# Moving every on-chip pool so that TensorE's operand rows begin at multiples of 128 bytes

## The chip, the core and the metric

The kernel runs on one NeuronCore of a Trainium2 chip. The metric is device time in microseconds of one execution, as the median of several timed runs; lower is better. The other seven cores are idle.

Each core has five engines that run their own instruction streams and meet at semaphores: TensorE (PE; matrix products, out of the on-chip memory SBUF into PSUM), VectorE (DVE), ScalarE (ACT), GpSimd (POOL) and SyncE (SP), which here only issues transfers. SBUF has 128 partitions; a tile of the program takes the same stretch of bytes in each of them. "Where a row begins" means the byte address within a partition.

## The reference, cut to what is computed

One block of a hybrid model on 512 tokens of width 1024, all in float32:

```python
h = rms_norm(x, norm1_g)
z, xbc, dt_raw, q, k, v, g_ssd, g_attn = split(h @ w_in)            # 12832 columns
y_ssd  = ssd_branch(z, xbc, dt_raw, ...)     # conv, state space in chunks of 128, gated norm
y_attn = attn_branch(q, k, v, ...)           # dilations 1, 4, 16; 8 heads of 64 in each
merged = sigmoid(g_ssd) * (y_ssd @ w_ssd_proj) + sigmoid(g_attn) * (y_attn @ w_attn_proj)
x  = x + merged @ w_out
h2 = rms_norm(x, norm2_g)
u_gate, u_val = split(causal_dwconv(h2 @ w_up))                     # 2 x 2816 columns
out = x + (silu(u_gate) * u_val) @ w_down
```

## The kernel before

**Products in three parts.** A float32 product is made of three float32r products: every operand is split into a high part (a copy rounded to float32r) and a low part (what is left), and high x high, high x low and low x high are added up in PSUM. The names show it: hh/hl (the normed input, transposed), ah/al (attention out), yh/yl (state space out), mh/ml (merged), h2h/h2l (second norm), acth/actl (feed-forward), whi/wlo (weights). Weights come as a stream of 194 pieces of 128 x 1024: load_piece (L85) issues the transfer into raw, make_piece (L91) splits it with one ScalarE copy (L100) and one VectorE subtraction (L101).

**Two forms of product.** In mm_chan (L135) the weights are the stationary operand, 128 columns wide, and the activations stream past as the moving one, 512 columns: the products of ps_ssd, ps_gate, ps_ap and ps_u (L140). The state space out-projection ps_sp (L855) has that form too. In proj_tok (L387, products at L393: ps_v, ps_qk) and mm_tok (L876, products at L882: ps_wo, ps_wd) it is the other way round: the activations are stationary and 512 weight columns move. In the trace's names the moving operand comes first: ps_ssd<-hl,whi streams hl past whi. For the second and third dilation tok (L382) reads the activations with a step of 4 tokens.

**Order.** TensorE's order is written by hand (manual_schedule, L147): attention projections by dilation, 8 groups of the state space branch, gates, the projections of the two branches, the output projection with the second norm, then the feed-forward. The smaller work (attention scores and values, transposes, state space chains) goes on in generators, one step at a tick, a tick being 12 products (L143 to L145, L455). Its products are float32 ones, not float32r: ps_s (L496), ps_pt, ps_pv, ps_tq, ps_st, ps_y, ps_o.

**Placement.** Pools are stacks: those of the left side grow up from const, those of side="right" grow down from the top. Within a pool a tile takes its bytes per partition, rounded up to 32. In the program as built, by address and by what is left over a multiple of 128:

| tiles | first byte | past a multiple of 128 |
|---|---|---|
| ident, ones, wd2 (const) | 16512, 17024, 22272 | 0 |
| triu, tril, sc (const) | 17632, 18144, 18656 | 96 |
| raw, whi, wlo (weights, after const ends) | 24736, 37024, 49312 | 32 |
| hh, hl; mh, ml; yh, yl; acth, actl; bct, xst, zs (left) | 72352, 88736; ... | 32 |
| ah, al, ysb; x1, h2h, h2l (right, from the top 229344 down) | 212960, 221152, 180192; ... | 96 |
| s, pt, gt, hn, junk (right, below those) | 167904, 174048, ... | 96 |
| kz, qt, vt, qr, mneg (right, below res4; 32 bytes) | 135104, 114880, 106688, ... | 64 |
| sr, sq, prev, xdt, xdc, btok, cbm, eb, bc (right, below two rv; 32 bytes each) | 173984, ... | 32 |

The rows of a tile are whole multiples of 128 bytes apart, and the slices that TensorE reads begin at multiples of 512 bytes within a tile (the step of 4 tokens in tok excepted: there they begin 0, 4, 8 or 12 bytes on). So all rows of a tile share its remainder.

Of the kernel before, what the change touches and what calls it, by code (L numbers as in the profile page):

```python
# [8 lines left out]
F32 = mybir.dt.float32  # L9
# [7 lines left out]
P = 128  # L17
S = 512
NT = S // P
# [1 line left out]
KD = D // P  # L21
EPS = 1e-6
NEG = -1.0e30
# Ticks (of 12 matrix products) between the steps of the work beside the weight products.
LAG, PVLAG, QLAG = 2, 2, 4      # attention: scores to transposes, those to values, head norms
LW = (3, 0, 0)                  # further wait of the attention of each dilation
COMB = 11                       # last attention chain to the combination of the dilations
G0, G1, GN = (2, 1, 1, 1), (5, 2, 4, 2), (7, 2, 2)  # state space groups: C.B, inputs, outputs
G2W, YL = 4, 3
NL = (1, 3, 2, 1)               # steps of a group's norm  # L30

Z0, XS0, B0, C0, DT0 = 0, 2048, 4096, 5120, 6144
Q0, K0, V0, GS0, GA0 = 6176, 7712, 9248, 10784, 11808
# [5 lines left out]
def kernel(  # L39
# [6 lines left out]
    nc = tc.nc  # L46
    x, out = x[0], out[0]
# [6 lines left out]
    def pool(name, side="left", bufs=1):  # L54
        return tc.tile_pool(name=name, bufs=bufs, side=side, reuse_waits="tile")

    cp = ctx.enter_context(pool("const"))
# [4 lines left out]
    def bank(tag, name):  # L62
        return pp.tile([P, 512], F32, tag=tag, name=name, bufs={"mm": 4, "tr": 2, "aux": 2}[tag])

    # ---- weights: a stream of pieces of 128 x 1024, each split into two float32r parts
    def chan_piece(w, c0, n, k0=0, nk=KD):
        return w[k0 * P:(k0 + nk) * P, c0:c0 + n].rearrange("(k p) c -> p k c", p=P)

    pieces = []
# [15 lines left out]
    def load_piece():  # L85
        n = len(raws)
        raw = wp.tile([P, pieces[n].shape[1], pieces[n].shape[2]], F32, tag="raw", name=f"raw{n}", bufs=3)
        nc.sync.dma_start(raw, pieces[n])
        raws.append(raw)
# [22 lines left out]
            make_piece()  # L112
        return made[i]

    # ---- work beside the matrix products: generators that go on at each tick
    sides = []

    def tick():
# [9 lines left out]
    def start(gen, wait=0):  # L128
        sides.append([gen, wait])
# [47 lines left out]
    scr_r = dp.tile([8, S], F32, tag="scr_r", name="scr_r")  # L177
    scr_f = dp.tile([24, S], F32, tag="scr_f", name="scr_f")

    comb_cm = pool("comb")  # L180
    comb = comb_cm.__enter__()
    hT_cm = pool("hT")
# [11 lines left out]
    def wide(b):  # L194
        return ysb[:, b:b + 2, :].rearrange("p a b -> p (a b)")

    # ---- first norm
    def rstd(ss, rs, n):
        nc.vector.tensor_scalar(ss, ss, 1.0 / n, EPS, op0=ALU.mult, op1=ALU.add)  # L199
        nc.gpsimd.tensor_tensor(rs, ss, nhalf.broadcast_to(tuple(ss.shape)) if ss.shape[1] > 1 else nhalf, op=ALU.pow)  # L200
# [13 lines left out]
    for t in range(NT):  # L214
        nc.sync.dma_start(wide(2 * t), x[t * P:(t + 1) * P, :])
        if t < 2:
            load_piece()
    # keeps TensorE busy until the first operands are there, so that its clock is up by then
    def warm(n, name):
        ps = bank("tr", f"ps_warm{name}")  # L220
        for i in range(n):
            nc.tensor.matmul(ps[:, :P], ones, ones, start=True, stop=True)
# [28 lines left out]
    def first_l(t, half):  # L251
        rest[t, half]()

    # ---- parameters by channel, on partitions
    def params():
        r1, r2, r3, r4 = (ysb[:n, 12, i * P:(i + 1) * P] for i, n in enumerate((128, 108, 88, 44)))
        nc.sync.dma_start(r1, ssd_conv_w[0].rearrange("k (b p) -> (k b) p", p=P))
        o = 0
        for v, n in ((ssd_conv_b, 32), (norm1_g, 8), (ssd_norm_g, 16), (norm2_g, 8), (ffn_conv_b, 44)):
            nc.sync.dma_start(r2[o:o + n, :], v[0].rearrange("(b p) -> b p", p=P))  # L260
            o += n
        nc.sync.dma_start(r3, ffn_conv_w[0, 0:2].rearrange("k (b p) -> (k b) p", p=P))
        nc.sync.dma_start(r4, ffn_conv_w[0, 2].rearrange("(b p) -> b p", p=P))
        for j, v in enumerate((q_norm_g, k_norm_g)):
            for i in range(2):
                nc.sync.dma_start(qkg[i * 64:(i + 1) * 64, j:j + 1], v[0].unsqueeze(1))
        for i in range(2):
            nc.sync.dma_start(dsk[i * 64:(i + 1) * 64, :],
                              d_skip[0].rearrange("(b i) -> i b", i=2)[i].partition_broadcast(64))
        yield 3  # L270
        nc.gpsimd.tensor_scalar(qkg[:, 0:1], qkg[:, 0:1], 0.125, None, op0=ALU.mult)
        ps = bank("tr", "ps_sc")
        o = 0
        for r, n in ((r1, 128), (r2, 108), (r3, 88), (r4, 44)):
            nc.tensor.transpose(ps[:, o:o + n], r, ident[:n, :n])
            o += n
        nc.vector.tensor_copy(sc, ps[:, :368])

    # ---- time steps: softplus, decays and their running sums
    def time_steps():  # L280
        def small(i):
            return ysb[:, 13, i * P:(i + 1) * P] if i < 4 else ysb[:, 15, (i - 4) * P:(i - 3) * P]
# [71 lines left out]
    start(params(), 1)  # L354
    start(time_steps(), 7)

    # ---- dilated window attention
    aa_cm = pool("attn_a", side="right")
    aa = aa_cm.__enter__()
    ab_cm = pool("attn_b", side="right")  # L360
# [2 lines left out]
    def masks():  # L363
        for j, src in enumerate((triu, tril)):
            nc.vector.tensor_scalar(mneg[:, j, :], src, -NEG, NEG, op0=ALU.mult, op1=ALU.add)
        res4 = aa.tile([P, 4], F32, tag="res4", name="res4")
        nc.vector.reduce_sum(res4, ident.rearrange("p (a b) -> p b a", b=4), axis=AX.X)
        nc.vector.tensor_mul(mneg[:, 2, :].rearrange("p (a b) -> p a b", b=4),
                             tril.rearrange("p (a b) -> p a b", b=4),
                             res4.unsqueeze(1).broadcast_to((P, 32, 4)))  # L370
        nc.vector.tensor_scalar(mneg[:, 2, :], mneg[:, 2, :], -NEG, NEG, op0=ALU.mult, op1=ALU.add)
        yield 1
# [85 lines left out]
    def norm_heads(which, g, b, ps):  # L458
        nm = f"{which}_{g}_{b}"
        qr = ab.tile([P, 512], F32, tag="qr", name=f"qr{nm}", bufs=4)  # L460
        nc.scalar.copy(qr, ps)
        sq = ab.tile([P, 512], F32, tag="qsq", name=f"qsq{nm}", bufs=1)
        nc.scalar.activation(sq, qr, AF.Square)
        ss = ab.tile([P, 8], F32, tag="qss", name=f"qss{nm}", bufs=4)
        nc.vector.reduce_sum(ss, sq.rearrange("p (h d) -> p h d", h=8), axis=AX.X)
        rs = ab.tile([P, 8], F32, tag="qrs", name=f"qrs{nm}", bufs=4)
        rstd(ss, rs, 64)

        def later():
            q3 = qr.rearrange("p (h d) -> p h d", h=8)  # L470
            nc.vector.tensor_mul(q3, q3, rs.unsqueeze(2).broadcast_to((P, 8, 64)))
            yield 1
            ps = bank("tr", f"ps_tq{nm}")
            for j in range(4):
                nc.tensor.transpose(ps[:, j * P:(j + 1) * P], qr[:, j * P:(j + 1) * P], ident)
            p3 = ps.rearrange("p (j t) -> p j t", j=4)
            bs = slice(b * P, (b + 1) * P)
            if which == 0:
                nc.scalar.activation(qts[g % 2][:, :, bs], p3, AF.Copy, scale=qkg[:, 0:1])
            else:  # L480
                nc.scalar.activation(kz[0:64, :, 0, bs], p3[0:64], AF.Copy, scale=qkg[0:64, 1:2])
                nc.vector.tensor_scalar(kz[64:128, :, 1, bs], p3[64:128], qkg[64:128, 1:2], None, op0=ALU.mult)
        start(later(), QLAG)
# [3 lines left out]
    def chain(g, j, b, nb):  # L487
# [38 lines left out]
        if b + nb == NT:  # L526
# [5 lines left out]
            if j == 3:  # L532
# [4 lines left out]
                if g == 2:  # L537
                    start(combine(), COMB)

# [59 lines left out]
    for g in range(3):  # L599
# [5 lines left out]
        for which in (0, 1):  # L605
            proj_tok(g, f"qk{which}{g}_", lambda b, ps: norm_heads(which, g, b, ps))
        start(launch(g), QLAG + LW[g])
        if g == 2:
            proj_v()

    # ---- state space branch
    sa_cm = pool("ssd_a")
    late = {}

# [20 lines left out]
    def ssd_side(g, bct, xst, zs, at):  # L635
        sp = late["b"]

        def T(tag, shape, bufs=1):
            return sp.tile(shape, F32, tag=tag, name=f"{tag}_{g}", bufs=bufs)
# [77 lines left out]
        nc.gpsimd.tensor_add(sq[:, 0, :], sq[:, 0, :], sq[:, 1, :])  # L717
        yield NL[0]
        sr = sp.tile([P, 2, S], F32R, tag="sr", name=f"sr_{g}", bufs=1)
        nc.scalar.copy(sr[:, 0, :], sq[:, 0, :])  # L720
        nc.gpsimd.tensor_sub(sr[:, 1, :], sq[:, 0, :], sr[:, 0, :].bitcast(F32))
        yield NL[1]
        ps = bank("aux", f"ps_n{g}")
# [3 lines left out]
        nc.scalar.activation(vv, ps[0:1, :], AF.Identity, bias=epsb[0:1], scale=1.0 / 256)  # L727
        nc.sync.dma_start(scr_v[g], vv)
        yield NL[2]
        rv = T("rv", [P, NT], 2)  # L730
        nc.sync.dma_start(rv, scr_v[g].rearrange("(p c) -> p c", c=NT))
        yield NL[3]
        nc.gpsimd.tensor_tensor(rv, rv, nhalf.broadcast_to((P, NT)), op=ALU.pow)
# [14 lines left out]
    for g in range(8):  # L748
        if g > 1:
            branch_tiles(g)  # L750
        if g > 1:
            start(ssd_side(g, *tiles[g], normal), G2W if g == 2 else 0)
# [30 lines left out]
                start(ssd_side(1, *branch_tiles(1), dict(zip(("cb", "x", "y"), G1))), G1[3])  # L783
                start(silus(*tiles[0]), 1)

    # ---- gates and projections of the two branches
    def gate(m, o):
        w = next_piece()
        ps = bank("mm", f"ps_gate{m}")
# [75 lines left out]
    yp_cm.__exit__(None, None, None)  # L865
    ap_cm.__exit__(None, None, None)

    # ---- output projection, residual and second norm
    x1_cm = pool("x1", side="right")
    x1p = x1_cm.__enter__()  # L870
    x1 = x1p.tile([P, NT, D], F32, tag="x1", name="x1")
# [32 lines left out]
    n2 = np_cm.__enter__()  # L904
    gb2 = n2.tile([P, D], F32, tag="gb2", name="gb2")
    nc.sync.dma_start(gb2, norm2_g[0].partition_broadcast(P))
    sums = n2.tile([P, NT, 2], F32, tag="sums", name="sums")

    def add_x1(nh, b, ps):
        cs = slice(nh * 512, (nh + 1) * 512)  # L910
# [61 lines left out]
        for i in range(2):  # L972
            mm_chan(up0[i], wu[i], h2h, h2l, t0=256, nt=256, ticks=False, lo_first=True)

    # ---- feed-forward
    ff_cm = pool("ffn")
    act_cm = pool("act")

# [69 lines left out]
```

## Time and profile before

| what | value |
|---|---|
| timed runs, median (lowest to highest) | 1248.98 us (1247.35 to 1249.27) |
| span of the profiled execution, first to last instruction | 1246.2 us (its own time is not listed apart) |
| TensorE busy | 1228.4 us, 99%, 5944 products |
| VectorE / ScalarE / GpSimd busy | 57% / 45% / 8% |
| mean granted TensorE clock over the span | 0.995 |
| transfers | 128.11 MB, 16 engines busy 35% of the span |

How to read it: TensorE's products are pipelined, so that two that follow each other overlap in the trace, and the mean duration of one is not its pace. The chain that ended last gives each instruction only the time by which it moved the end, so that a long piece of the chain, divided by the number of its products, is the pace. Stages by time: attention projections up to 296 us, state space 297 to 629, gates to 723, ps_ap to 745, ps_sp to 832, ps_wo to 877, ps_u to 1123, ps_wd to the end.

### The profile page before, as it was taken

To read this page: it belongs to the slowest core of one execution; us is meant where nothing else is said; L and a number is where in the kernel's file an instruction comes from. 1 tells how busy PE (TensorE), PEld (TensorE's weight loads), DVE (VectorE), ACT (ScalarE), POOL (GpSimd) and SP (SyncE) were. 2 spreads that over 40 slices of the span, in tenths; PEclk is the share of its full clock that TensorE was granted. 3 is DMA by queue.
4 is the path that set the end of the run, shared out by engine and by line. 5 is a ranking of instruction groups with operands and counts; after the bars stand their busy time and mean duration, and the time that the engine had idled before them with its cause. 6 is when DMAs were issued, how large, how long until landed. Compare 5 with 4: busy or idle time off the path is not lost.

```text
span 1246.2 us, 15060 instructions
## 1 busy us (share of the span) xinstructions
PE 1228.4 (99%) x5944; PEld 1025.2 (82%) x5944; DVE 713.2 (57%) x956; ACT 557.6 (45%) x848; POOL 95.1 (8%) x71
## 2 busy tenths in 40 slices
PE   8799999999999999999999999999999999999998
PEld 6579888898788888888888888888888888888887
DVE  4255455655588988777743553653766566563222
ACT  3334454646766555655433233432544444442210
POOL 2022022220000101110102000000000000000000
PEclk9899999999999999999999999999999999999999
DMA  4333212113445644344333523343233332332340
GB/s 158 106 85 88 69 52 69 51 53 85 131 125 162 182 116 123 100 135 118 86 81 89 167 86 102 101 170 101 85 98 89 102 98 88 102 100 87 110 127 34
DMA packets 154829, 128.11 MB, mean 103 GB/s; under 512 B 12662, under 2 KB 125926, under 8 KB 153735
## 3 DMA queue, kind: packets, MB, share of 16 engines
q1 hardware_dynamic: 154759, 127.15, 34.9%
q8 instruction: 47, 0.77, 0.3%
q14 instruction: 23, 0.19, 0.1%
HBM read 124.72 MB, written 2.41 MB: 102 GB/s over the span
## 4 chain that ended last, share of the span: by engine, by line
PE 90%; DVE 3%; DMA 3%; ACT 1%; POOL 1%; issue 1%; SPq 0%; DVEq 0%; POOLq 0%; ACTq 0%
PE ps_u L140 19%; PE ps_ssd L140 18%; PE ps_qk L393 10%; PE ps_wd L882 10%; PE ps_gate L140 7%; PE ps_sp L855 7%; PE ps_v L393 5%; PE ps_wo L882 3%; PE ps_s L496 2%; PE ps_ap L140 2%; PE ps_pv L523 1%; PE ps_pt L512 1%; PE ps_y L703 1%; DMA ysb<-in_w_in_dram 1%; PE ps_o L708 1%; DMA dsk<-in_d_skip_dram 1%
## 5 line engine op out<-in xcount | busy, mean ns | idle before, releaser
L101 DVE TENSOR_TENSOR wlo<-raw,whi 128x1024 fp32r<-128x1024 f32 x194 | 244.1, 1259 | 330.4 <-ACT whi L100 204.6
L100 ACT CAST whi<-raw 128x1024 fp32r<-128x1024 f32 x194 | 203.3, 1049 | 319.5 <-PE ps_wd L882 79.8
L140 PE MATMUL ps_ssd<-hl,whi 128*128 128x512 f32 x384 | 103.4, 398 | 0.0
L140 PE MATMUL ps_ssd<-hh,whi 128*128 128x512 f32 x384 | 98.6, 399 | 0.0
L140 PE MATMUL ps_ssd<-hh,wlo 128*128 128x512 f32 x384 | 95.3, 390 | 0.0
L140 PE MATMUL ps_u<-h2h,whi 128*128 128x512 f32 (+1 forms) x368 | 88.7, 383 | 0.3 <-ACT h2h L209 0.2
L140 PE MATMUL ps_u<-h2h,wlo 128*128 128x512 f32 (+1 forms) x368 | 88.1, 382 | 0.0
L140 PE MATMUL ps_u<-h2l,whi 128*128 128x512 f32 (+1 forms) x368 | 88.0, 381 | 0.0
L140 PEld LDWEIGHTS ps_ssd<-hh,wlo 128*128 128x128 f32 x384 | 72.1, 188 | 15.8
L140 PEld LDWEIGHTS ps_ssd<-hh,whi 128*128 128x128 f32 x384 | 71.0, 188 | 14.3 <-issue 0.2
L140 PEld LDWEIGHTS ps_ssd<-hl,whi 128*128 128x128 f32 x384 | 70.4, 188 | 13.9 <-issue 0.5
L140 PEld LDWEIGHTS ps_u<-h2h,whi 128*128 128x128 f32 x368 | 67.2, 188 | 14.5 <-ACT h2h L209 0.8
L140 PEld LDWEIGHTS ps_u<-h2l,whi 128*128 128x128 f32 x368 | 67.2, 188 | 13.9
L140 PEld LDWEIGHTS ps_u<-h2h,wlo 128*128 128x128 f32 x368 | 67.2, 188 | 13.7
L393 PE MATMUL ps_qk<-whi,hh 128*128 128x512 f32 x192 | 69.4, 443 | 0.0
L52 DVE SCALAR_TENSOR_TENSOR facc<-ps_u,sc,facc 128x511 f32<-128x511 f32 x88 | 65.8, 747 | 5.8 <-ACT facc L981 4.3
L200 POOL TENSOR_TENSOR qrs<-qss,nhalf 128x8 f32<-128x8 f32 x24 | 46.3, 1927 | 214.7 <-DVE qss L199 214.7
L393 PE MATMUL ps_qk<-whi,hl 128*128 128x512 f32 x192 | 60.3, 395 | 0.0
L393 PE MATMUL ps_qk<-wlo,hh 128*128 128x512 f32 x192 | 60.2, 395 | 0.0
L507 ACT ACTIVATE s<-s,st 128x128 f32<-128x128 f32 (+1 forms) x96 | 40.0, 418 | 36.1 <-DVE st L503 35.9
L882 PE MATMUL ps_wd<-whi,actl 128*128 128x512 f32 x176 | 54.2, 389 | 0.0
L882 PE MATMUL ps_wd<-wlo,acth 128*128 128x512 f32 x176 | 54.2, 389 | 0.0
(237 smaller groups left out, 2103.8 us busy)
## 6 DMA issues: line engine op xcount, KB each, us to landing
raw<-in_w_in_dram SPq DMA_DIRECT2D x100, 512.0 KB, 3.9
raw<-in_w_up_dram SPq DMA_DIRECT2D x44, 512.0 KB, 3.8
raw<-in_w_down_dram SPq DMA_DIRECT2D x22, 512.0 KB, 3.8
bc<-scr_a SPq DMA_DIRECT2D x8, 1024.0 KB
raw<-in_w_ssd_proj_dram SPq DMA_DIRECT2D x16, 512.0 KB, 3.8
eb<-scr_e SPq DMA_DIRECT2D x16, 256.0 KB, 6.3
raw<-in_w_out_dram SPq DMA_DIRECT2D x8, 512.0 KB, 4.3
fb<-scr_f SPq DMA_DIRECT2D x24, 128.0 KB, 2.9
```

The costliest lines, as they stand in the source:

```text
L52: nc.vector.scalar_tensor_tensor(o, a, s, b, op0=op0, op1=op1)
L100: nc.scalar.copy(hi, raw)
L101: nc.vector.tensor_sub(lo, raw, hi.bitcast(F32))
L140: nc.tensor.matmul(ps[:, t0:t0 + nt], a[:, k, c:c + n], b[:, k, t0:t0 + nt], start=(i == 0), stop=(i == total - 1))
L200: nc.gpsimd.tensor_tensor(rs, ss, nhalf.broadcast_to(tuple(ss.shape)) if ss.shape[1] > 1 else nhalf, op=ALU.pow)
L393: nc.tensor.matmul(pss[b], tok(g, kq * 2 + k, b, xx), w[:, k, :], start=(kq == 0 and j == 0 and k == 0), stop=(kq == 3 and j == 2 and k == 1))
L496: nc.tensor.matmul(ps[:, i * 2 * n:(i + 1) * 2 * n], qt[:, j, (b + i) * P:(b + i + 1) * P], kz[:, j, :, k0 + i * P:k0 + i * P + n], start= ...
L507: nc.scalar.activation(s3[:, 2 * i + h], s3[:, 2 * i + h], AF.Exp, bias=st[:, b + i, 0, 2 * j + h:2 * j + h + 1], accum_out=st[:, b + i, 1 ...
L512: nc.tensor.transpose(pst[:, o:o + P], s[:, o:o + P], ident)
L523: nc.tensor.matmul(pso[h * 64:(h + 1) * 64, (b + i) * P:(b + i + 1) * P], vt[:, b + i - nk + 1 + kb, (2 * j + h) * 64:(2 * j + h + 1) * 64 ...
L855: nc.tensor.matmul(pss[j], w[:, k, cs], ys[k][xi], start=(k2 == 0 and i == 0 and k == 0), stop=(k2 == 7 and i == 2 and k == 1))
L882: nc.tensor.matmul(pss[b], xx[:, k0 + k, b * P:(b + 1) * P], ww[:, k, :], start=(k0 == 0 and j == 0 and k == 0), stop=(k0 == nk - 2 and j ...
```

## The change

Pads are put into the pools and three small tiles are widened. edge_l lies in const, ahead of all that the left side holds; edge_r is the first tile from the top of the right side. Both are 24 floats (96 bytes) for each partition and are filled with zeros by GpSimd; nothing reads them. res4, rv and sums get rows of 128 bytes (rv and res4 are used in the same first columns as before; of sums the same 4 x 2 elements are used). Lines of comment are removed, which moves line numbers. Nothing else changes: the same instructions in the same order on each engine, with other addresses.

```diff
+    edge_l = cp.tile([P, 24], F32, tag="edge_l", name="edge_l")
+    nc.gpsimd.memset(edge_l, 0.0)
+    edge = ctx.enter_context(pool("edge", side="right"))
+    edge_r = edge.tile([P, 24], F32, tag="edge_r", name="edge_r")
+    nc.gpsimd.memset(edge_r, 0.0)
+
     comb_cm = pool("comb")
...
-        res4 = aa.tile([P, 4], F32, tag="res4", name="res4")
+        res4 = aa.tile([P, 32], F32, tag="res4", name="res4")[:, 0:4]
...
-        rv = T("rv", [P, NT], 2)
+        rv = T("rv", [P, 32], 2)[:, 0:NT]
...
-    sums = n2.tile([P, NT, 2], F32, tag="sums", name="sums")
+    sums = n2.tile([P, 4 * NT, 2], F32, tag="sums", name="sums")
```

## Rows read from the trace of the kernel before

**Rows 1.** Page, part 1: busy us, share of the span, instructions.

```profile
PE 1228.4 (99%) x5944; PEld 1025.2 (82%) x5944; DVE 713.2 (57%) x956; ACT 557.6 (45%) x848; POOL 95.1 (8%) x71
```

**Rows 2.** Page, part 4: the chain that ended last, by engine.

```profile
PE 90%; DVE 3%; DMA 3%; ACT 1%; POOL 1%; issue 1%; SPq 0%; DVEq 0%; POOLq 0%; ACTq 0%
```

**Rows 3.** TensorE's waits: line, releaser; us in total, times, longest.

```profile
PE ps_v L393 <- ACT hh L209: 10.8, 1, 10.8
PE ps_warma L222 <- DVE epsb L157: 1.1, 1, 1.1
PE ps_s L496 <- DVE s L501: 0.7, 1, 0.7
...
PE ps_st L684 <- DVE xdc L678: 0.4, 1, 0.4
```

**Rows 4.** Chain that ended last, at the start: start us, us, what.

```profile
26.26 12.17 DMA ysb<-in_w_in_dram
```

**Rows 5.** The same chain: long pieces of products alone, with their count.

```profile
49.77 8.16 PE ps_qk L393 x36
...
74.95 3.63 PE ps_dt L299 x16
...
668.84 54.43 PE ps_gate L140 x240
723.27 21.99 PE ps_ap L140 x96
745.26 87.09 PE ps_sp L855 x384
...
886.20 236.66 PE ps_u L140 x1056
1122.87 119.71 PE ps_wd L882 x528
```

**Rows 6.** Timeline of TensorE, ps_u of 256 columns: start us, us, what.

```profile
879.34 1.10 PE L140 MATMUL ps_u<-h2h,wlo 128*128 128x256 f32 x8
880.28 1.11 PE L140 MATMUL ps_u<-h2l,whi 128*128 128x256 f32 x8
```

**Rows 7.** Windows: us, busy by engine (instructions), granted clock, DMA share, GB/s.

```profile
400.00:500.00 100.00, 99.60 (x545) 81.21 (x544) 86.75 (x115) 55.61 (x63) 13.51 (x9) 1.00 0.52 143
...
296.70:629.30 332.60, 332.11 (x1779) 270.66 (x1778) 261.02 (x343) 195.08 (x252) 29.30 (x20) 1.00 0.45 124
629.30:723.20 93.90, 93.90 (x446) 77.06 (x445) 40.43 (x49) 31.70 (x39) 9.17 (x7) 1.00 0.41 113
723.20:745.20 22.00, 22.00 (x98) 18.04 (x97) 12.99 (x17) 7.69 (x11) 0.00 (x0) 1.00 0.28 96
```

**Rows 8.** Chain that ended last: float32 score products of 256 columns.

```profile
300.26 0.87 PE ps_s L496 x4
```

**Rows 9.** Groups by form, one of three alike: count, busy us, mean ns.

```profile
L140 PE MATMUL ps_ssd<-hl,whi 128*128 128x512 f32 x384 | 103.4, 398 | 0.0
...
L140 PE MATMUL ps_u<-h2h,whi 128*128 128x512 f32 x336 | 83.9, 392 | 0.0
...
L140 PE MATMUL ps_gate<-hl,whi 128*128 128x512 f32 x128 | 32.1, 391 | 0.0
...
L882 PE MATMUL ps_wo<-whi,ml 128*128 128x512 f32 x64 | 19.7, 389 | 0.0
...
L724 PE MATMUL ps_n<-sr,ones_r 128*1 128x512 f32 x8 | 3.2, 397 | 0.0
```

**Rows 10.** Timeline of TensorE, third dilation, strided weights: start us, us, what.

```profile
206.73 0.63 PE L393 MATMUL ps_qk<-wlo,hh 128*128 128x512 f32 x2
207.20 0.63 PE L393 MATMUL ps_qk<-whi,hh 128*128 128x512 f32 x2
```

**Rows 11.** Timeline of GpSimd at the start: start us, us, what, idle before.

```profile
0.79 0.20 POOL masks.py:197 MEMSET ident<- 128x128 f32 x1 [0.29 <-POOLq L1035]
...
6.04 0.56 POOL L200 TENSOR_TENSOR rs<-ss,nhalf 128x1 f32<-128x1 f32 x1 [0.58 <-DVE ss L199]
6.54 0.09 POOL L287 MEMSET dtb<- 64x1 f32 x1
```

## The prediction

> **What bounds the kernel now.** I read the page's busy shares first [rows 1]: TensorE 99%, VectorE 57%, ScalarE 45%, GpSimd 8%. The chain that ended last is TensorE for 90% of the span, in the weight products [rows 2]. A busy TensorE may still wait inside its share, so I read its waits next [rows 3]: 10.8 us in one wait at the start, for hh, and under 1 us in any other place after that. The start is a matter of transfers (the chain's piece of 12.17 us from w_in [rows 4]); from 40 us on the time is the number of products times the pace of one. So the pace decides, and I took it from long unbroken pieces of the chain [rows 5], a piece's time divided by its count, since the mean duration of one matmul (about 390 ns) holds a pipeline's overlap.
>
> Those pieces fall into two kinds. Moving rows on the left side (hh, whi, yh, mh) give 119.71/528 = 226.7 ns, 87.09/384 = 226.8, 54.43/240 = 226.8 and 8.16/36 = 226.7. Moving rows on the right side (ah, h2h) give 21.99/96 = 229.1 ns; the 236.66 us of ps_u hold 1008 products of 512 columns and 48 of 256 columns, and with 117.5 ns for each of the latter (0.94 us for 8 [rows 6]) the others take 229.2. ps_gate and ps_ap have the same shape, the same loop and weights from the same buffers; what differs is where the moving row begins: 32 bytes past a multiple of 128 on the left, 96 past one on the right. The placement of the pools is added up in the section on the kernel. So the trace already shows that the pace hangs on the start, and that at neither start it is the 213.3 ns that 512 columns would take at one for each period of the 2.4 GHz level (the clock was granted at 1.00 in these stretches [rows 7]).
>
> What part of the 226.7 is the start? Two rows narrow it. In ps_dt [rows 5] the weights (wd2) are 64 columns wide instead of 128 and begin at a multiple of 128 already, while the moving rows are hh: 3.63/16 = 226.9 ns. So neither the weights' start nor their length sets the pace; the moving row is left. And the f32 products of ps_s, with 256 columns in an instruction, take 0.87/4 = 217.5 ns [rows 8]: that is 512 periods too (two for each column) with 4 ns on top, though their moving rows (kz) begin 64 bytes past. At half the speed of reading the loss is not there. The left-hand pace is 543.9 to 544.3 periods, which is 512 x 17/16 = 544: a row of 2048 bytes holds 16 blocks of 128 bytes and, begun off the block, reaches into 17, and 1/16 more time is what every block paying for a second one would cost. That is a reading of one number, not shown by any row here, since no float32r row of this kernel begins on a block.
>
> **The change part by part.**
> 1. Pads. In const, edge_l adds 96 bytes: the weights begin at 24736 + 96 = 24832 = 194 x 128, and everything left of the middle follows in multiples of 128. On the right edge_r takes 96 bytes at the top: 229344 - 96 = 229248 = 1791 x 128, so ah, al, ysb, x1, h2h and h2l begin on a block. res4, rv and sums grow to 128 bytes, so what lies below them (kz, qt, vt, s, pt; the state space tiles; gb2, hn) does too. By addition the change does what it says, but for triu, tril and sc, which no weight product reads, and the token-strided weights of the second and third dilation, whose rows begin 0, 4, 8 or 12 bytes past a block.
> 2. Pace after it. The ends: 213.3 ns (nothing lost), and 226.7 (this is the pace whatever the start); beyond that the slower rival below. I take 216, 2.7 ns over 512 periods, nearest to ps_s [rows 8], whose 217.5 includes changes of weights between two kinds of work. The Trainium skill, "TensorE: Matmul & The Clock Gate", section "Back-to-back issue gap", gives 518 cycles for 512 columns, 215.8 ns at 2.4 GHz; the trace before is 11 ns above it, and by it the sum below would be 1 us larger.
> 3. The count [rows 9]. Each row there is one of three alike. Left, with weights read in a run: 3 x 384 of ps_ssd, 3 x 128 of ps_gate, 384 of ps_sp, 3 x 64 of ps_wo, 528 of ps_wd, 16 of ps_dt, 16 of ps_n (sr lies on the right, but 32 past as well), and of the first dilation's 288 products those behind the opening wait, some 228: 2,900 x 10.8 ns = 31.3 us. The 576 of the second and third dilation run at 235 ns (0.47 us for two [rows 10]); their weights are read at a stride, which the change leaves, so I give them the same 10.8 ns: 6.2 us. Right: 3 x 336 of ps_u and 96 of ps_ap: 1,104 x 13.2 = 14.6 us. The 96 of 256 columns: 117.5 to 109 (half of 213.3 and 2.3): 0.8 us. Sum 52.9 us. All of it lies on TensorE, which is the path; the 2 us or so of the opening products lie in the shadow of the transfer and count for nothing. The f32 products and the transposes I leave as they are.
> 4. What gives some back. The work beside the products goes by ticks of 12 products, so its steps come 5% closer together while VectorE's and ScalarE's instructions stay as long as they are. The tightest stretch is 400 to 500 us, where VectorE is busy 86.75 of 100 us [rows 7]; with 4.7% less time it is 91%, still below TensorE. Over the whole state space stretch it is 261.02 of 332.60. After the start, TensorE's waits come to 2 us [rows 3]; I let them double: 2 us given back. At worst the whole state space stretch gains nothing: 1152 x 10.8 ns = 12.4 us.
> 5. Two fills of 128 x 24 on GpSimd. The rows nearest are 0.09 us (64 x 1) and 0.20 us (128 x 128) [rows 11]: 0.2 to 0.4 us for both. Queued behind them are the first norms' powers; the first stood 0.58 us idle for VectorE, which covers them. If that cover were gone, 0.4 us before the opening transfer, which hides it again. res4, rv and sums stay as many elements as they were in every instruction; no transfer, wait or queue is moved. The pads shift the two sides by 96 to 192 bytes towards each other, and the tiles that share memory one after another share it with the same ones as before.
>
> Sum: the profiled execution's span is 1246.2 us, 2.8 us below the median 1248.98 (the program's ends lie around it; a profiled time of its own is not given). 1246.2 - 52.9 + 2 = 1195.3 us of span, and with 2.8 around it 1198 us.
>
> **The rivals.**
> - Starts at multiples of 32 are all alike and 226.7 ns is what a float32r product of 512 columns costs. For: the steadiness of 226.7 over four stages; against: 229.1 and 229.2 at the other start. Then only the right side could gain, 229.2 to 226.7: 1,104 x 2.5 = 2.8 us, 1246 us. 0.10. The trace as it stands allows this.
> - Nothing moves at all: the 2.4 ns on the right come from something else than the start, and the time is 1249 us. 0.15. What would do it here: a row is fetched in pieces so short that 32 and 96 are both whole pieces, then no fetch is split before or after. The Trainium skill, "Advanced Engine Details and Errata", section "SBUF Cachelines", says that SBUF has lines of 16 bytes and that further accesses to the same line are at full performance; every start here is a multiple of 16, so by that rule the time stays at 1249 us. The trace speaks against it with its two paces for the two starts.
> - Slower. The pace is no steady function of the start: 226.7 at 32, 229.2 at 96, and 0 may lie on the far side, by the same step of 2.5 ns: 229.2 on the left too, about 3,500 x 2.5 = 8.7 us, 1257 us. Its place would be every product whose moving row and weight row begin together on a block; it decides once the pace of ps_wd is above 226.7. Against it: on the left both rows begin 32 past a block today, so beginning together does not hurt by itself. 0.09.
> - The gain is there and the side work eats it: VectorE late in the state space stretch. That is the 12.4 us of point 4: 1198 + 10 = 1208 us. It is within the forecast's own range.
>
> **How the numbers follow.** The forecast, pace near 216, has 0.66: 1198 us, by itself 1191 (the strided products lose their extra too, 576 x 8 ns = 4.6 us, and no wait is added) to 1211. The rivals have 0.10 (1246), 0.15 (1249) and 0.09 (1257). About 0.2% is what a measurement of this kernel can tell from no change, 2.5 us. The right-side case is just outside it, so most of its 0.10 goes to faster: 0.74 faster, 0.17 same, 0.09 slower. The range goes from 1190 to 1248: out of it are the slower case, the half of no change that would lie above 1248, and a little of the forecast, together 0.2.
>
> **What would show it.** After the change ps_wd's 528 products in some 114 us instead of 119.71, ps_sp's 384 in 83 instead of 87.09, ps_u without a difference to the left side; ps_s at 217 as before; ps_dt like the others. If ps_wd stays at 226.7 the reading of 17/16 is wrong; if ps_wd falls and the state space stretch does not, point 4 is. If the span falls by the sum but waits of TensorE appear, the pace fell below 216.

## The result and the profile after

The changed kernel takes 1252.71 us (median; 1251.65 to 1253.53) against 1248.98 us before (1247.35 to 1249.29). The ratio on record is 1.0037 with a 95% interval of 1.0024 to 1.0049, and by the two medians alone it is 1.0030: 0.3 to 0.4% slower, where 4% faster was forecast. The span of the profiled execution is 1249.9 us, 3.7 us more than before.

The chain that ended last in the changed kernel, long pieces of products alone (start us, us, what), to be laid beside [rows 5]:

```profile
50.21 8.16 PE ps_qk L400 x36
...
75.39 3.68 PE ps_dt L306 x16
...
668.69 54.42 PE ps_gate L140 x240
723.12 22.39 PE ps_ap L140 x96
745.51 87.05 PE ps_sp L862 x384
...
886.45 240.21 PE ps_u L140 x1056
1126.66 119.70 PE ps_wd L889 x528
```

The pieces of ps_qk, ps_gate, ps_sp and ps_wd take what they took, to 0.04 us, although every row they read now begins on a block of 128 bytes: 226.7 ns for a product, not 216. ps_u takes 3.55 us more and ps_ap 0.40 us more. Their sum, 3.95 us, is the loss (the rest of the span comes out 0.2 us shorter). The products of ps_u and ps_ap, 1,104 of them with the full 512 columns, read a moving row on the right side.

TensorE's waits in the changed kernel (line, releaser; us in total, times, longest), the counterpart of [rows 3]:

```profile
PE ps_v L400 <- ACT hh L216: 11.8, 1, 11.8
PE ps_warma L229 <- DVE epsb L157: 1.1, 1, 1.1
PE ps_s L503 <- DVE s L508: 0.7, 1, 0.7
```

No new wait came in. The opening one is 1.0 us longer, but the start of the first ps_qk piece moved by 0.44 us only (49.77 us before), and in the experiments below it lies anywhere between 49.26 and 51.05 us. TensorE has the same work in the same order; in two stages, ps_ap and ps_u, each product is slower.

GpSimd's start in the changed kernel (timeline: start us, us, what, idle before), the counterpart of [rows 11]:

```profile
0.93 0.12 POOL L182 MEMSET edge_l<- 128x24 f32 x1
0.98 0.12 POOL L185 MEMSET edge_r<- 128x24 f32 x1
1.16 1.80 POOL L383 MEMSET kz<- 64x2048 f32 x1
...
6.25 0.56 POOL L207 TENSOR_TENSOR rs<-ss,nhalf 128x1 f32<-128x1 f32 x1 [0.67 <-DVE ss L206]
```

The two fills move the kz fill by 0.11 us (it began at 1.05 us), and the first power still waits for VectorE, as forecast.

### The profile page after: what moved, and what is told of

It is laid out like the page before. It is cut to its first block, busy times and chain, and to the rows that moved or that the text cites. A ratio compares the mean times of both kernels' runs of the same rounds, so it can differ in the third digit from the quotient of the medians.

```text
span 1249.9 us, 15062 instructions
## 1 busy us (share of the span) xinstructions
PE 1231.7 (99%) x5944; PEld 1025.0 (82%) x5944; DVE 713.9 (57%) x956; ACT 557.8 (45%) x848; POOL 94.4 (8%) x73
## 4 chain that ended last, share of the span: by engine, by line
PE 96%; DVE 1%; DMA 1%; ACT 1%; POOL 1%; issue 0%; POOLq 0%; ACTq 0%; DVEq 0%
PE ps_ssd L140 21%; PE ps_u L140 20%; PE ps_qk L400 10%; PE ps_wd L889 10%; PE ps_gate L140 7%; PE ps_sp L862 7%; PE ps_v L400 5%; PE ps_wo L889 3%; PE ps_s L503 2%; PE ps_ap L140 2%; PE ps_pv L530 1%; PE ps_y L710 1%; PE ps_pt L519 1%; PE ps_o L715 1%; DMA ysb<-in_w_in_dram 1%; PE ps_st L691 1%
## 5 line engine op out<-in xcount | busy, mean ns | idle before, releaser
L140 PEld LDWEIGHTS ps_u<-h2h,wlo 128*128 128x128 f32 x368 | 67.4, 188 | 14.8
L140 PEld LDWEIGHTS ps_u<-h2l,whi 128*128 128x128 f32 x368 | 67.4, 188 | 14.8
L889 PE MATMUL ps_wd<-whi,acth 128*128 128x512 f32 x176 | 54.2, 389 | 0.0
```

The lines of the kernel that those rows point to most:

```text
L140: nc.tensor.matmul(ps[:, t0:t0 + nt], a[:, k, c:c + n], b[:, k, t0:t0 + nt], start=(i == 0), stop=(i == total - 1))
L889: nc.tensor.matmul(pss[b], xx[:, k0 + k, b * P:(b + 1) * P], ww[:, k, :], start=(k0 == 0 and j == 0 and k == 0), stop=(k0 == nk - 2 and j ...
```

## The experiments

What was open: why shifting h2h and the weights by 96 bytes each changes the pace of ps_u, when shifting hh and the weights by 96 bytes each changes nothing in ps_gate. Three theories: PLACE (where the moving row lies), DISTANCE (how far moving row and weight row are apart) and COMPANY (what the other engines do meanwhile). BLOCK is the recorded reading, that a row begun on a multiple of 128 bytes is read faster.

**1. Products alone (m1_products_alone).** One large float32r tile, filled once; then groups of 48 products in which the byte where the moving row and the weight row begin is set by hand, rows 2048 and 512 bytes apart as in mm_chan. All groups ran twice, the second time in reverse order.

```diff
+    # name, moving row, weight row (bytes), step of moving, step of weights, columns moved, weight columns
...
+    ('upbef', 196576, 37024, 2048, 512, 512, 128),
+    ('upaft', 196480, 37120, 2048, 512, 512, 128),
+    ('upleft', 196576, 37120, 2048, 512, 512, 128),
...
+    ('uptwok', 196608, 37120, 2048, 512, 512, 128),
...
+    ('wtshigh', 72448, 213120, 2048, 512, 512, 128),
...
```

> Products alone, with no other engine at work: 29 groups of 48 float32r products (two passes, the second in reverse order), each with its own place of the moving row and of the weight row, the rest of the block left out (the output is not the block's). What the case's own traces say: rows on the left run at 226.7 ns at 32 and at 0 past a multiple of 128; h2h on the right runs at 229.2 before and 232.4 after. Theory PLACE (the pace hangs on where the moving row lies in SBUF): groups with the moving row at 196480 and above run at 229 to 233 ns whatever the weights' place, groups below at 226.7, also at 4, 16, 32, 64 and 96 bytes past a block. Theory DISTANCE (it hangs on how far moving row and weight row are apart): shifting the weights alone (upleft, bothhigh, wtshigh) changes the pace as much as shifting the moving row. Theory COMPANY (other engines' reads and writes in the feed-forward stretch slow ps_u): every group runs at 226.7 here, the high ones too. Theory BLOCK (the recorded prediction): groups at multiples of 128 run at 216 ns, the others at 227.

The chain of this kernel, first pass (start us, us, what; 48 products in a piece, so 10.88 us is 226.7 ns and 11.20 us is 233.3; the clock was granted at 1.00 here):

```profile
126.98 11.15 PE ps_upaft L98 x48
138.14 11.20 PE ps_upleft L98 x48
...
160.52 10.93 PE ps_uptwok L98 x48
171.45 11.19 PE ps_downmid L98 x48
182.65 11.00 PE ps_downbef L98 x48
...
204.53 10.88 PE ps_lowb L98 x48
...
248.73 11.20 PE ps_pastthirtytwo L98 x48
259.93 11.00 PE ps_pastsixtyfour L98 x48
...
282.14 10.89 PE ps_bothhigh L98 x48
293.03 11.19 PE ps_wtshigh L98 x48
304.22 10.92 PE ps_wtsmid L98 x48
...
348.43 11.09 PE ps_narrow L98 x48
359.52 11.04 PE ps_narrowlow L98 x48
370.56 5.69 PE ps_half L98 x48
376.25 5.75 PE ps_halflow L98 x48
382.00 10.38 PE ps_bfl L98 x48
```

COMPANY falls: the slow pace is there with no other engine at work. PLACE falls: uptwok lies as high as upaft and is fast; wtshigh has its moving row as low as the gates' and is slow. BLOCK falls: upaft, downmid and wtshigh begin on blocks, both rows of them, and are slow. What sorts the groups is moving row minus weight row, taken modulo 256. It is 0 for uptwok (159488 = 623 x 256), lowb, wtsmid and bothhigh; 128 for upaft, downmid and wtshigh; 64 for downbef and pastsixtyfour; 224 for upleft; 32 for pastthirtytwo.

ps_halflow (256 columns, distance 0) gives 5.75/48 = 119.8 ns against 226.7 for 512 columns. The difference, 106.9 ns, is 256 columns at the 2.4 GHz level (106.7). So at distance 0 what a float32r product costs over its columns is some 13 ns once for each product, and not 1/16 of the reading time. At distance 128 it is another picture: ps_half (256 columns) takes 5.69/48 = 118.5 ns, 12 ns over its columns, and upaft (512) 232.3 to 233.3, some 20 ns over them. With 256 columns distance 0 is thus not the faster one.

**2. One pad at a time (e1_left_pad_alone, e2_right_pad_alone).**

```diff
 # e1: the changed kernel without edge_r
-    edge_r = edge.tile([P, 24], ...)
...
 # e2: the changed kernel without edge_l
-    edge_l = cp.tile([P, 24], ...)
...
```

> The changed kernel without edge_r: weights and all of the left side begin on blocks of 128, the right side stands where it stood before (h2h at 196576, 96 past). PLACE: ps_u and ps_ap as before, 229.2 ns, the time within 1248 to 1250 us. DISTANCE: the distance from weights to h2h changes by 96 bytes, so ps_u moves off 229.2. BLOCK: the left products at 216, 1215 us; but the trace of the changed kernel already speaks against it.

> The changed kernel without edge_l: the right side on blocks (h2h at 196480), weights and left side at 32 past as before. PLACE: ps_u at 232.4 ns as in the changed kernel, some 1252.5 us. DISTANCE: the distance from weights to h2h differs by 96 bytes both from before and from the changed kernel, so ps_u may take a third pace. COMPANY: no forecast between 229 and 233.

Measured: 1253.78 us, ratio 1.0040 (1.0028 to 1.0053), and 1252.63 us, 1.0032 (1.0020 to 1.0044). The times alone can't tell a third pace from the changed kernel's; the stage can. Each pad alone brings h2h to a distance of 159456 = 622 x 256 + 224 bytes from the weights. The chain of e1_left_pad_alone, and of e2_right_pad_alone below it:

```profile
724.73 22.40 PE ps_ap L140 x96
...
888.04 241.16 PE ps_u L140 x1056
```

```profile
723.56 22.40 PE ps_ap L140 x96
...
886.88 241.16 PE ps_u L140 x1056
```

One has left rows on blocks and right rows off them, the other the reverse; their ps_u agree to 0.01 us, and differ from before (236.66) and from the changed kernel (240.21). DISTANCE alone allowed a third pace. In e1 h2h did not move at all and became slower.

**3. The distance, byte by byte (m2_distance_scan).** Products alone again.

```diff
+    ('dnought', 72448, 37120, 2048, 512, 512, 128),
+    ('dfour', 72452, 37120, 2048, 512, 512, 128),
...
+    ('bothfour', 72452, 37124, 2048, 512, 512, 128),
...
+    ('bfsixteen', None, 8, 0, 0, 512, 128),
...
+    ('stepsb', 37120, 72452, 2048, 2048, 512, -4),
...
```

The moving row is at 72448 + d, the weight row at 37120, for 20 values of d from 0 to 252; then come both rows moved together by 4, 16, 64 and 128 bytes, bf16 at d = 0, 16, 64 and 128, and six groups with weights at a step of 4 elements.

> Products alone again, the rest of the block left out. Groups of 48 with the moving row d bytes further past a multiple of 256 than the weight row (d = 0 to 252), four groups with both rows moved together by 4, 16, 64 and 128 bytes (d = 0), four of bf16 at d = 0, 16, 64 and 128, and six with weights read at a step of 4 elements as the second and third dilation do. Theory DISTANCE MOD 256: d = 0 gives 226.7 ns, 64 gives 228.9 or 233.3, 128 gives 232 to 233.4, all others 231 to 235, and the both groups 226.7 whatever the start. Theory DISTANCE AND BLOCK: the both groups at 4 and 16 bytes are slower than 226.7, since a start off 32 bytes costs too. For bf16 neither theory has a row yet but 215.8 at d = 0: if the loss belongs to 4-byte reads alone, it is 215.8 at every d.

The chain, a few pieces of the first and of the second pass (dnought is d = 0, and so on; "both" groups have d = 0):

```profile
238.37 10.88 PE ps_dtwohundredforty L109 x48
...
260.29 11.47 PE ps_bothfour L109 x48
271.76 11.05 PE ps_bothsixteen L109 x48
282.81 10.89 PE ps_bothsixtyfour L109 x48
...
325.36 10.36 PE ps_bfsixtyfour L109 x48
...
460.08 11.28 PE ps_stepsb L109 x48
...
579.61 11.35 PE ps_dtwohundredforty L109 x48
...
658.25 11.14 PE ps_dhundredtwentyeight L109 x48
...
702.79 10.99 PE ps_dsixtyfour L109 x48
...
780.80 10.92 PE ps_dnought L109 x48
```

A piece's time through 48, in ns, first and second pass (in the first, the big tile was still being filled up to 124 us, so up to d = 64; of d = 0 it has only products that had not settled):

| d | ns | d | ns | d | ns |
|---|---|---|---|---|---|
| 0 | not settled / 227.5 | 64 | 228.8 / 229.0 | 176 | 233.3 / 233.3 |
| 4 | 235.8 / 234.8 | 80 | 231.3 / 231.0 | 192 | 233.1 / 233.3 |
| 8 | 233.1 / 233.3 | 96 | 233.5 / 233.3 | 208 | 234.6 / 234.6 |
| 12 | 230.2 / 230.0 | 112 | 231.3 / 231.3 | 224 | 233.3 / 233.1 |
| 16 | 231.7 / 231.7 | 128 | 232.3 / 232.1 | 240 | 226.7 / 236.5 |
| 32 | 233.3 / 233.3 | 144 | 233.3 / 233.3 | 252 | 229.8 / 230.0 |
| 48 | 233.1 / 233.3 | 160 | 234.2 / 234.4 | | |

0 is the only distance that is fast whenever it had settled, here and in both passes of experiment 1; 64 (the kernel before) is next of those that kept their pace here, and 128 (the changed kernel) is 3 ns behind that. My expectation that the start is of no account at d = 0 failed below 64 bytes: with both rows 16 past it is 230.2 and 233.1 ns, with both 4 past 239 ns. At 64 and 128, and at the 32 that the kernel before has, it holds. bf16 is at 10.36 to 10.38 us, 216 ns, at all four distances: the loss was seen with float32r products alone.

**4. The distance mended, in two ways and with the blocks kept (e3_right_64, e5_left_64, e4_blocks_and_distance).**

```diff
 # e3: the kernel before
+    edge_r = edge.tile([P, 16], ...)        # 64 bytes, right side; h2h 0 from the weights, 32 past a block
 # e5: the kernel before
+    edge_l = cp.tile([P, 16], ...)          # 64 bytes, in const; h2h 0 from the weights, 96 past a block
 # e4: the changed kernel
-    edge_r = edge.tile([P, 24], ...)
+    edge_r = edge.tile([P, 56], ...)        # 224 bytes; h2h 0 from the weights, on a block
```

The lines for a pad's pool and its fill are left out, here and in experiment 5.

> The kernel before with one pad, 64 bytes at the top of the right side: h2h goes to 196512 and stands 0 past a multiple of 256 from the weights (64 before, 128 in the changed kernel); every row still begins 32 past a block of 128. DISTANCE MOD 256: ps_u at 226.7 ns, its 236.66 us become 234.1, ps_ap 21.8, the time 2.8 us below the kernel before, 1245.5 us. BLOCK or PLACE: no gain, 1248 to 1250 us.

> The kernel before with one pad, 64 bytes in const on the left: the weights go to 37088, h2h stays at 196576, the distance is 0 past a multiple of 256 again, now by moving the other operand; rows begin 96 past a block on both sides. DISTANCE MOD 256: the same 1245.5 us as with the right pad. PLACE: ps_u as before, 229.2 ns, 1248.5 us.

> The changed kernel with edge_r of 224 bytes in place of 96: every operand row begins on a block of 128 as in the changed kernel, and h2h (196352) stands 0 past a multiple of 256 from the weights (37120). DISTANCE MOD 256: ps_u 234.1 us, all of the loss undone and more, 1245.5 us. If starting on a block costs something by itself: still above the kernel before.

Measured: 1245.64 us, ratio 0.9981 (0.9972 to 0.9990); 1246.02 us, 0.9986 (0.9977 to 0.9995); 1246.25 us, 0.9988 (0.9979 to 0.9997). All three beat the kernel before, by 0.1 to 0.2% with intervals that end below 1; among themselves their times can't be told apart. The chains of e3_right_64, then e4_blocks_and_distance, then e5_left_64:

```profile
722.92 21.76 PE ps_ap L140 x96
...
885.64 234.54 PE ps_u L140 x1056
```

```profile
725.34 21.76 PE ps_ap L140 x96
...
888.04 234.53 PE ps_u L140 x1056
```

```profile
887.01 234.53 PE ps_u L140 x1056
```

ps_u is 234.5 us whether rows begin on a block (e4) or off it (e3), and whichever side was moved (right in e3, left in e5). Against the changed kernel e4 moves the right side by another 128 bytes and nothing else: every row is still on a block, and 5.7 us of ps_u are gone.

**5. The loss without the alignment, and the same loss elsewhere (e7_right_128_unaligned, e6_left_apart_128).**

```diff
 # e7: the kernel before
+    edge_r = edge.tile([P, 48], ...)        # 192 bytes, right side: h2h 128 from the weights, 32 past a block
 # e6: the kernel before
+    edge_r = edge.tile([P, 32], ...)        # 128 bytes, left side, after the weights: hh, yh, mh, acth 128 from them
```

> The kernel before with one pad of 192 bytes on the right: h2h at 196384 stands 128 past a multiple of 256 from the weights, as in the changed kernel, but no row begins on a block of 128 (32 past on both sides). DISTANCE MOD 256: ps_u 240.2 us as in the changed kernel, 1252.5 us: the change's whole loss without its alignment. If starting on a block has a part in the loss: below that.

> The kernel before with one pad of 128 bytes on the left, between the weights and all that follows: hh, yh, mh and acth stand 128 past a multiple of 256 from the weights instead of 0, while every row still begins 32 past a block of 128 and the right side stands where it stood. DISTANCE MOD 256: ps_gate, ps_sp, ps_wo, ps_wd go from 226.7 to 232.2 to 233.4 ns, ps_wd's 119.7 us become 122.6 to 123.2, and with some 2,900 products slowed by 5.5 to 6.7 ns, and 576 strided ones by about 4, the time is 18 to 22 us above the kernel before, 1266 to 1270 us; ps_u stays at 236.7. BLOCK or PLACE: no change, since remainders to 128 are as before.

Measured: e7 1251.94 us, ratio 1.0030 (1.0020 to 1.0040); e6 1262.56 us, 1.0115 (1.0098 to 1.0132). The chain of e7, then of e6:

```profile
725.86 22.39 PE ps_ap L140 x96
...
889.17 240.22 PE ps_u L140 x1056
1129.39 119.70 PE ps_wd L886 x528
```

```profile
678.44 55.77 PE ps_gate L140 x240
734.21 21.98 PE ps_ap L140 x96
756.19 89.22 PE ps_sp L859 x384
900.15 236.66 PE ps_u L140 x1056
1136.81 122.71 PE ps_wd L886 x528
```

e7 has the changed kernel's ps_u to 0.01 us with no row on a block. In e6 the left stages that the change had left alone slow down (ps_wd 122.71/528 = 232.4 ns, ps_gate 232.4, ps_sp 232.3) and the right ones stay as before. The whole came to 14.8 us of loss instead of 18 to 22. Part of the gap is in the interrupted stages: in the state space stretch a piece of 12 products between two steps of the side work goes from 2.75 to 2.79 us, 3 ns for a product, not 5.7. One such piece, before and in e6:

```profile
511.80 2.75 PE ps_ssd L140 x12
```

```profile
518.78 2.79 PE ps_ssd L140 x12
```

The starts of the single products in the two traces show where it goes. Behind an interruption of the state space stretch the second to fourth products take 232 ns on average before and 231 in e6; the fifth to eleventh take 228.7 and 232.9. The distance begins to count only when a stream has run for a few products.

## Why the prediction was wrong, point by point

**What bounds the kernel** held: TensorE's pace and nothing else sets the end from 40 us on, no new wait came in, and the whole difference is a count of products times a change of pace.

**The step that failed** is the reading of the pace, "what differs is where the moving row begins", and with it the value taken for the pace after the change. ps_gate and ps_ap [rows 5] differ in the moving row's start; the distance from that row to the weight row differs with it, 0 against 64 past a multiple of 256 bytes, and I didn't work it out, though both addresses stand in the table of the placement. The start made no difference to this pace where both rows were on multiples of 32 bytes: e4 against e3 and e5, and e7 against the changed kernel, show ps_u equal on and off a block.

**The 17/16** was a coincidence, and there was a row against it: in 512 x 17/16 the extra grows with the columns. At distance 0 it is some 13 ns at 256 columns as at 512 (experiment 1). The 256-column products of ps_u [rows 6] took 117.5 ns where 256 x 17/16 columns would take 113.3, and I used them only for the count. The ps_dt row, which was to leave the moving row alone, compared weights of another width (64 columns) at another distance (160); the narrow groups of experiment 1 run at 11.04 us for 48 at distance 0 and 11.09 at 128, 230 and 231 ns, by other paces than the full ones. In the changed kernel ps_dt stands at distance 0 and is not faster for it: 3.68/16 = 230.0 ns against 226.9. And ps_s at 217.5 ns is not the same product without the loss: it is a float32 product, and 256 columns of float32r take 119.8 ns (experiment 1), not 217.5.

**The sum.** Of its terms the left side (31.3 and 6.2 us) came to nothing, because the weights and the rows that go with them shift together there: the distance is 0 before and after (72352 - 37024 = 138 x 256 for hh). The right side (14.6 us of gain) became 3.95 us of loss, since its pad went the other way from the left one: 159552 = 623 x 256 + 64 became 159360 = 622 x 256 + 128. The sign turned on 192 bytes of distance. What I had granted for the fills was right and small; the 2 us for the side work were not put to the test, since the products beside it came no closer together.

**The rivals.** "Slower" named the sign and the size of a step (2.5 ns; it was 3.5 for ps_u, 3.55 us over its 1,008 products of full width) but put it on the left, for rows that begin on a block. Its own argument against itself, that rows beginning together do not hurt on the left, was half of the answer: they help. "Starts at multiples of 32 are all alike and 226.7 is what a product costs" was right for distance 0. The Trainium skill's rule of 16-byte lines ("Advanced Engine Details and Errata", section "SBUF Cachelines") made the change worth nothing. The measurement decides against it twice: ps_u lost 3.55 us, and both rows 16 bytes past and both rows 64 past, alike by that rule, took 11.05 and 10.89 us for 48. The 518 cycles, 215.8 ns, that the Trainium skill gives for 512 columns ("TensorE: Matmul & The Clock Gate", section "Back-to-back issue gap") are met by the bf16 groups (10.36/48 = 215.8 ns) and by no float32r group of 512 columns.

**What was to show it** worked: ps_wd at 119.70 us instead of 114 was the line named beforehand for a wrong 17/16, and it is the first line to read in the profile after.

## What to carry to other kernels

When a pace differs between two stages, list everything that differs between their operands, distances included, before naming one; two addresses give two starts and a distance, and only a test that moves both together separates them. With long streams of float32r products of 512 columns and weights 128 columns wide, put the moving row and the weight row a multiple of 256 bytes apart and start both on multiples of 32 bytes (0, 32, 64 and 96 past a block were run): here that was worth 1.2% when lost on the left stages and 0.2% when won on the right ones. A pad of 64 bytes, chosen by the difference of two addresses, did what pads to an absolute alignment could not.

## What the runs showed of the hardware that was not expected

The pace of a stream of float32r products is not one number but a repeating pattern that depends on what ran before. At d = 240 the same 48 products took 10.88 us in one pass and 11.35 in the other; in the trace the starts of the single products follow each other by 226, 227, 227 ns over and over in the first pass, and by 234 and 239 in turn in the second. At d = 64 the pattern is 226, 229, 232 ns in experiment 3 and in the kernel before; but behind another group, upbef of experiment 1 kept to 233, 233, 234 in its second pass and took 11.19 us, 233.1 ns for a product instead of 229. So some distances have two paces, and each lasted to the end of its 48 products. Weights that are read at a step of 4 elements run at 235 to 237 ns at distance 0 (11.28 and 11.36 us for 48) and at 239.5 ns at 64 and 128 bytes from it (11.49 and 11.50 us for 48; 23.00 for 96): the distance counts there too, but 0 does not bring them to 226.7.

Why the distance counts modulo 256 is open. The trace shows weight loads running under the products (188 ns each in the float32r groups, while TensorE has no gap). That the two reads get into each other's way would fit, and that bf16, at half the bytes and 98 ns for a load, shows nothing would fit too; no run here took the weight loads away (onewt, with the same weights each time, still loads them, 188 ns each), so it is argued, not shown. Where the 13 ns of a float32r product at distance 0 come from is open as well.
